# A two-layer FFN and token-mix trunk on one core: sub-layer ends without GpSimd, decay tables on VectorE, preparation spread out

## The chip, the cores and the metric

The kernel runs on one core of a Trainium2 chip. The metric is the device time of one execution in microseconds (us), the median over the runs shown. The engines are TensorE (PE in the rows; PEld is its weight load), VectorE (DVE), ScalarE (ACT), GpSimd (POOL) and SyncE (SP), which here only issues DMAs. The profiled execution is a separate one.

## The reference, cut to what matters

Two layers work on 256 latent tokens and 256 context tokens of width 1024. Each layer is an FFN, a token mix and another FFN; each of the three has a norm before it, a modulation, and a gated residual with a second norm behind it. The vectors of the modulation come from the matrices `w_ada`.

```python
def modulated_norm(xs, gain, mod, s):
    return rms_norm(xs, gain) * (1.0 + mod_vec(mod, 3 * s + 1)) + mod_vec(mod, 3 * s)

def gated_residual(xs, y, gain, mod, s, weight):
    return xs + weight * mod_vec(mod, 3 * s + 2) * rms_norm(y, gain)

def ffn_sublayer(xs, mod, s, g_pre, g_post, w_in_f, w_out_f):
    a, g = jnp.split(modulated_norm(xs, g_pre, mod, s) @ w_in_f, 2, axis=-1)
    return gated_residual(xs, (jax.nn.silu(a) * g) @ w_out_f, g_post, mod, s, MACARON_WEIGHT)
...
for l in range(DEPTH):
    xl = ffn_sublayer(xl, mod_l, 0, ...)          # latents
    xc = ffn_sublayer(xc, mod_c, 0, ...)          # context
    yl, yc = token_mix(modulated_norm(xl, ...), modulated_norm(xc, ...), ...)
    xl = gated_residual(xl, yl, norm_post[l, 1], mod_l, 1, 1.0)
    xl = ffn_sublayer(xl, mod_l, 2, ...)
    if not last:                                  # the last layer's mix and second FFN keep the latents only
        xc = gated_residual(xc, yc, norm_post[l, 1], mod_c, 1, 1.0)
        xc = ffn_sublayer(xc, mod_c, 2, ...)
return xl
```

One of the four branches of the token mix is a state-space model (S5). It needs tables of powers of a complex decay and of their products with the matrices B and C, which depend on the parameters alone, not on the tokens.

## The kernel before

**Tokens and precision.** The tokens lie in four tiles of 128 rows: tiles 0 and 1 are the latents (`st` 0 in the norm), tiles 2 and 3 the context (`st` 1). Every matmul is in three products of a high and a low part (`mm3`, L282 to L287): each operand is split into a part rounded to fp32r and what is left over. The low part is the subtraction `wlo` or `hTlo` in the rows.

**Weights.** `K.W` is a ring (`Ring`): two places for raw weights of 1 MB, loaded from SP's queue, and three places for their halves. `ahead(n)` splits further weights until `n` places ahead are filled: the high half on ScalarE (L208), or on VectorE (L210) if `K.hi_eng` is set; the low half on `K.lo_eng` (L211), which is VectorE except where the end of a sub-layer sets GpSimd. A call of `ahead` thus puts a ScalarE cast and a subtraction into the order of the engines where it stands.

**Order.** Each engine works through its instructions in program order; the order is written out by hand. `K.clock` is a planned clock that the matmul groups advance by `tick`. A `Task` is a generator; its `yield` gives the planned time after which it emits its next stretch. Two tasks matter here: `Ada`, the modulation vectors, and `s5_prep`, the preparation of the S5 tables of a layer during its first FFN. `finish` emits what is left of a task at once.

**The norm before a sub-layer** (`PreNorm`): `square` takes sums of squares on ScalarE, `stats` the reciprocal root, `scale` writes `xs` on VectorE (L433), `transpose` brings it to PSUM on TensorE (L292), and `modulate` applies scale and shift on ScalarE (L459), or on VectorE (L457), casts the high part on VectorE (L462) and subtracts the low part (L463) on the engine that its argument `los` names for each half.

**The end of a sub-layer** (`natural_out`) is the output projection, two column halves wide. In the second half the last weight pieces are held back, so that the tiles end one after the other: `part(ps, s, t)` multiplies one piece for tile t, `first(t)` begins the norm of the result, `update(ts)` finishes the residual and takes the squares for the next norm. The latents' norm is emitted between the context's parts; the context's norm (`ctx_norm`) at the start of the next sub-layer. With two tiles (before the last FFN) the same is done with no context to cover it. `nh` is the number of held pieces, 5 after an FFN and 4 after a mix.

**Preparation** (`s5_discretize` for both layers, within layer 0; `s5_load`; `s5_prep`). `s5_load` issues nine DMAs on two queues, `d1` and `d2`. `s5_prep` then builds, for each group `qg` of four, the table `rt` on VectorE, the table `x` (`p_xr`, `p_xi`) on GpSimd, which TensorE transposes, and for `qg` 0 and 1 the decay table F (`p_F`) in six doubling steps m = 1 to 32, each one complex product (`cmul`, six operations). The tables go to DRAM by DMAs on GpSimd's queue.

**Startup** (in `trace`): the first modulation vectors are computed through `Ada` with the weights in places borrowed from other tiles; the norm of the latents follows, then that of the context.

Stages of the profiled execution: startup to 62 us, first FFN to 469, mix to 910, second FFN to 1320; layer 1: first FFN to 1732, mix to 2014, second FFN (latents only) to the end.

Of the kernel before, what the change touches and what calls it, by code (L numbers as in the profile page):

```python
# [8 lines left out]
F32 = mybir.dt.float32  # L9
# [5 lines left out]
P = 128  # L15
# [450 lines left out]
def natural_out(K, y1, lhi, llo, nk, wview, tiles, G, nxt, hold, free):  # L466
# [55 lines left out]
    for h in range(2):  # L522
# [16 lines left out]
            continue  # L539
        if nxt is not None:  # L540
            pn = nxt()
        lo_eng = K.lo_eng
        if len(tiles) == 2:
            if pn is not None:
                K.lo_eng, K.hi_eng = nc.gpsimd, v
            subs = [piece(i, h, min(K.W.nsub - 1, n - 1 - len(hold) - i)) for i in range(n - nh, n)]
            for t in tiles:
                for j, s in enumerate(subs):
                    part(pss[t], s, t)
                    if t == 1 and pn is not None:  # L550
                        K.W.ahead(min(j, K.W.nsub - 1))
                first(t)
                update([t])
            if pn is not None:
                pn.stats(0)
                for q in range(2):
                    pn.scale(0, q)
                    pn.transpose(0, q)
                for q in range(2):
                    pn.modulate(0, q, (v, nc.gpsimd))  # L560
        else:
            subs = []
            for i in range(n - nh, n):
                subs.append(piece(i, h, min(K.W.nsub - 1, n - 1 - i)))
                part(pss[0], subs[-1], 0)
            K.lo_eng = nc.gpsimd
            first(0)
            update([0])
            for s in subs:
                part(pss[1], s, 1)  # L570
            first(1)
            K.W.ahead(0)
            update([1])
            pn.stats(0)
            pn.scale(0, 0)
            pn.scale(0, 1)
            for s in subs:
                part(pss[2], s, 2)
            K.W.ahead(K.W.nsub - 1)
            first(2)  # L580
            update([2])
            for i, s in enumerate(subs):
                part(pss[3], s, 3)
                if i == nh - 4:
                    pn.transpose(0, 0)
                    pn.modulate(0, 0, (nc.gpsimd, v))
                if i == nh - 3:
                    pn.transpose(0, 1)
                    pn.modulate(0, 1, (nc.gpsimd, v))
            first(3)  # L590
            update([3])
            pn.stats(1)
        K.lo_eng, K.hi_eng = lo_eng, None
    return pn


def ctx_norm(K, pn):

    for h in range(2):
        pn.scale(1, h)  # L600
        pn.transpose(1, h)
    for h in range(2):
        pn.modulate(1, h, (K.nc.vector, K.nc.gpsimd))


class FfnPools:
# [16 lines left out]
def ffn(K, l, s, f, pn, tiles, nxt, jobs, every=(5.0, 7.6), pools=None, prep=False):  # L623
# [8 lines left out]
    with pools.es as es:  # L632
# [29 lines left out]
            nc.vector.tensor_tensor(out=hid(1, 2 * c + n), in0=g[:, :N], in1=hh.bitcast(F32), op=OP.subtract)  # L662

        for i, (c, part, n) in enumerate(blocks):
            if c == 5 and part == 0 and n == 0:
                if ptask is not None:
                    finish(K, ptask)
                pstack.close()
                pb = es.enter_context(K.tc.tile_pool(name=f"hidB{l}{f}", bufs=1))
                hb = [pb.tile([P, 11, N], F32R, tag=f"hb{k}", name=f"hb{k}") for k in range(2)]  # L670
# [287 lines left out]
def s5_discretize(K, pool, sd):  # L958
# [37 lines left out]
    si = small.tile([P, 2, G2], F32, "p_si")  # L996
    fl = lambda t: t.rearrange("p a g -> p (a g)")
    for _ in zip_longest(exp_exact(nc, small, fl(mag), fl(arg[:, 0]), 2 * G2), sincos(nc, small, fl(co), fl(si), fl(arg[:, 1]), 2 * G2)):
        yield 2.5
    for l in range(2):  # L1000
        nc.gpsimd.dma_start(K.r8d[l], mag[:, 1, 16 * l:16 * l + 16])
    yield 2.5
# [65 lines left out]
def s5_prep(K, l, pool, tab, loads=None):  # L1068
# [9 lines left out]
    if l == 0:  # L1078
        yield from s5_discretize(K, pool, sd)
    else:  # L1080
        dq.dma_start(sd, K.sd)
        loads.append(s5_load(K, l, pool, dq, nc.scalar))
        yield 9.0
    sd = sd[:, :, 16 * l:16 * l + 16]
    pw = sd[:, 0:18, :].rearrange("p (m k) g -> p m k g", k=2)
# [38 lines left out]
    for qg in range(4):  # L1124
# [8 lines left out]
        if qg < 2:  # L1133
            g8 = slice(8 * qg, 8 * qg + 8)
            F = T([P, 8, 2, 64], "p_F")
            v.memset(F[:, :, 0, 0:1], 1.0)
            v.memset(F[:, :, 1, 0:1], 0.0)
            for k in range(6):
                m = 1 << k
                bc = lambda c: fms[k][:, c, g8].unsqueeze(2).to_broadcast([P, 8, m])  # L1140
                cmul(*((g_, pool) if m >= 16 else (v, pool)), F[:, :, 0, m:2 * m], F[:, :, 1, m:2 * m], F[:, :, 0, 0:m], F[:, :, 1, 0:m],
                     bc(0), bc(1), [P, 8, m], "p_cmg" if m >= 16 else "p_cmv")
                if k == 3:
                    yield 2.5
            yield 2.5 if qg == 0 else 11.0
            dq.dma_start(tab[:, g8, 640:768], F.rearrange("p g k n -> p g (k n)"))
        else:
            yield 5.0
# [489 lines left out]
def trace(K, nc, tc, rec):  # L1638
# [4 lines left out]
    with ExitStack() as es:  # L1643
# [43 lines left out]
        for l in range(2):  # L1687
# [2 lines left out]
        pn = PreNorm(K, 0, 0)  # L1690
        pools = FfnPools(K, 0, 0, 4, True)
        K.tasks.clear()
        ada = Ada(K, [h[:, 4 * j:4 * j + 4, :].rearrange("p (i a) b -> p i (a b)", i=2) for h in pools.hidden(F32) for j in range(2)],
                  [(0, 0, "norm", None)])
        for i, _ in enumerate(ada.run((0.0, 0.0), mm_tile)):
            if i == 0:
# [13 lines left out]
        pools.loads.append(s5_load(K, 0, pools.prep, nc.sync, nc.sync))  # L1710
        K.clock = 5.0
        for h in range(2):
            pn.modulate(0, h, (nc.gpsimd, nc.vector), (1,))
            K.W.ahead(1 + h)
        for t in range(2, 4):
            for h in range(2):
                pn.square(t, h)
        pn.stats(1)
        K.tasks.append(pools.ptask)
        for l in range(2):  # L1720
            last = l == 1
# [76 lines left out]
```

## Time and profile before

| | us |
|---|---|
| median of three runs | 2229.19 |
| lowest and highest run | 2224.33, 2229.96 |
| profiled execution | 2226.91 |
| its span, first to last instruction | 2225.1 |

The mean granted clock of TensorE over the span is 0.985 of full speed. Times within the span count from its first instruction. Between the profiled execution and its span lie 1.8 us.

### The profile page before, as it was taken

How to read it: one execution, taken by the hardware profiler on the slowest of the kernel's cores; microseconds unless marked ns; L12 is line 12 of the kernel's file. 1: busy time of each engine (PE TensorE's matmuls, PEld its weight loads, DVE VectorE, ACT ScalarE, POOL GpSimd, SP SyncE). 2: the span in 40 equal slices, each digit the busy share in tenths (PEclk: the TensorE clock that was granted, in tenths of full speed). 3: DMA queues.
4: the chain of work that ended last, by engine and by line, in shares of the span. 5: the costliest groups of instructions: out<-in, count | busy, mean ns of one | idle time of the engine just before them, and what ended most of it. 6: DMA issues, size and time to landing. Idle time of an engine off the chain costs nothing.

```text
span 2225.1 us, 28922 instructions
## 1 busy us (share of the span) xinstructions
PE 2120.0 (95%) x11691; PEld 1711.0 (77%) x11691; DVE 1121.9 (50%) x1965; ACT 764.2 (34%) x1275; POOL 391.6 (18%) x364
## 2 busy tenths in 40 slices
PE   5899999989999999899999999999999889997998
PEld 3677778878867778777777887678888778887997
DVE  5984332357435654533333356733324685756554
ACT  3222222332533334422222332222223345454443
POOL 1461000022222300100000026500000234432000
PEclk8999999999999999999999999999999999999999
DMA  8466543334322223355554335643223544443554
GB/s 296 152 218 213 203 148 104 129 109 153 105 72 71 82 73 116 124 174 189 185 183 155 105 110 183 221 147 120 85 86 110 183 149 143 126 142 127 178 190 150
DMA packets 214110, 323.12 MB, mean 145 GB/s; under 512 B 15736, under 2 KB 156664, under 8 KB 213976
## 3 DMA queue, kind: packets, MB, share of 16 engines
q1 hardware_dynamic: 196864, 287.17, 38.7%
q0 software_dynamic: 8432, 27.37, 3.8%
q10 hardware_dynamic: 8680, 6.73, 1.1%
q8 instruction: 92, 1.51, 0.3%
q14 instruction: 42, 0.34, 0.0%
HBM read 307.57 MB, written 14.71 MB: 145 GB/s over the span
## 4 chain that ended last, share of the span: by engine, by line
PE 46%; DVE 7%; issue 2%; ACT 2%; POOL 1%; DMA 1%; ACTq 0%; DVEq 0%; POOLq 0%
PE mm L285 14%; PE mm L287 14%; PE mm L286 14%; PE aux L341 2%; PE aux L292 1%; DVE wlo L211 1%; DVE xs L433 1%; ACT jk L400 1%; DVE at_mx L1415 0%; DVE hTlo L463 0%; DVE hThi L462 0%; ACT at_p L1424 0%; DVE mrg L890 0%; POOL p_F L110 0%; DVE g_tm L1597 0%
## 5 line engine op out<-in xcount | busy, mean ns | idle before, releaser
L285 PE MATMUL mm<-hThi,whi 128*128 128x512 f32 (+1 forms) x1992 | 719.4, 361 | 14.3 <-DVE hThi L462 8.8
L286 PE MATMUL mm<-hTlo,whi 128*128 128x512 f32 (+1 forms) x1992 | 703.4, 353 | 7.2 <-POOL hTlo L463 6.8
L287 PE MATMUL mm<-hThi,wlo 128*128 128x512 f32 (+1 forms) x1992 | 702.0, 352 | 2.0 <-DVE wlo L211 2.0
L211 DVE TENSOR_TENSOR wlo<-wraw,whi 128x1024 fp32r<-128x1024 f32 (+1 forms) x285 | 361.4, 1274 | 422.1 <-ACT whi L208 420.3
L285 PEld LDWEIGHTS mm<-hThi,whi 128*128 128x128 f32 x1992 | 382.4, 192 | 124.5 <-issue 50.3
L208 ACT ACTIVATE whi<-wraw 128x1024 fp32r<-128x1024 f32 (+1 forms) x348 | 363.6, 1048 | 237.1 <-PE mm L287 171.3
L286 PEld LDWEIGHTS mm<-hTlo,whi 128*128 128x128 f32 x1992 | 382.4, 192 | 57.2 <-POOL hTlo L463 9.6
L287 PEld LDWEIGHTS mm<-hThi,wlo 128*128 128x128 f32 x1992 | 382.0, 192 | 53.3 <-DVE wlo L211 2.8
L211 POOL TENSOR_TENSOR wlo<-wraw,whi 128x1024 fp32r<-128x1024 f32 (+1 forms) x66 | 161.3, 2453 | 847.8 <-ACT whi L208 799.0
L655 ACT ACTIVATE sa<-mm 128x512 f32<-128x512 f32 (+1 forms) x88 | 47.8, 543 | 244.7 <-PE mm L287 243.7
L659 DVE TENSOR_TENSOR sa<-sa,mm 128x512 f32<-128x512 f32 (+1 forms) x88 | 54.3, 617 | 151.1 <-PE mm L287 151.1
L285 PE MATMUL mm<-whi,ha 128*128 128x512 f32 x308 | 120.0, 389 | 0.0
L286 PE MATMUL mm<-wlo,ha 128*128 128x512 f32 x308 | 119.8, 389 | 0.0
L287 PE MATMUL mm<-whi,ha 128*128 128x512 f32 x308 | 119.8, 389 | 0.0
L661 ACT ACTIVATE ha<-sa 128x512 fp32r<-128x512 f32 (+1 forms) x44 | 25.4, 578 | 223.9 <-DVE sa L659 223.4
L661 ACT ACTIVATE hb<-sa 128x512 fp32r<-128x512 f32 (+1 forms) x44 | 25.4, 578 | 178.3 <-DVE sa L659 169.8
L287 PE MATMUL mm<-whi,hTlo 128*128 128x512 f32 (+2 forms) x224 | 80.6, 360 | 4.4 <-POOL hTlo L463 4.3
L285 PE MATMUL mm<-whi,hThi 128*128 128x512 f32 (+2 forms) x224 | 81.2, 363 | 3.3 <-DVE hThi L462 3.3
L286 PE MATMUL mm<-wlo,hThi 128*128 128x512 f32 (+2 forms) x224 | 79.5, 355 | 1.2 <-DVE wlo L211 1.2
L388 POOL DMA_DIRECT2D gd<-ev x12 | 7.0, 582 | 388.4 <-ACT whi L208 230.3
L285 PE MATMUL mm<-whi,hb 128*128 128x512 f32 x188 | 73.1, 389 | 0.0
L286 PE MATMUL mm<-wlo,hb 128*128 128x512 f32 x188 | 73.1, 389 | 0.0
(445 smaller groups left out, 2903.2 us busy)
## 6 DMA issues: line engine op xcount, KB each, us to landing
wraw<-in_w_ffn_in_dram SPq DMA_DIRECT2D x88, 1024.0 KB, 5.1
wraw<-in_w_in_dram SPq DMA_DIRECT2D x42, 1024.0 KB, 5.3
wraw<-in_w_ffn_out_dram SPq DMA_DIRECT2D x40, 1024.0 KB, 5.2
adaG<-in_w_ada_dram SPq DMA_DIRECT2D x32, 1024.0 KB, 5.0
aday<-in_w_ada_dram SPq DMA_DIRECT2D x32, 1024.0 KB, 5.0
ha<-in_w_ada_dram SPq DMA_DIRECT2D x8, 1024.0 KB, 7.5
wraw<-in_w_out_dram SPq DMA_DIRECT2D x7, 1024.0 KB
r_tq<-tab SPq DMA_DIRECT2D x8, 768.0 KB, 9.0
```

Source lines behind the costliest of these rows:

```text
L208: K.nc.scalar.activation(h3, r, AF.Copy)
L211: (self.eng or K.lo_eng).tensor_tensor(out=l3, in0=r, in1=h3.bitcast(F32), op=OP.subtract)
L285: mm(out, ahi, bhi, start=first, stop=False)
L286: mm(out, ahi, blo, start=False, stop=False)
L287: mm(out, alo, bhi, start=False, stop=last)
L292: K.nc.tensor.transpose(out, x, K.ident[:n, :n])
L341: nc.tensor.matmul(ps[o:o + 32, :], self.K.sc[:, k + i, :], w[:, i, 512 * b:512 * b + 512], start=k == 0, stop=k == 6, tile_position=(0, o))
L400: K.nc.scalar.activation(jk[:, :src.shape[-1]], src, AF.Square, scale=1.0 / 32.0, accum_out=acc)
L433: K.nc.vector.tensor_scalar(out=xs, in0=K.x[:, 2 * st + t, 512 * h:512 * h + 512], scalar1=self.rst[st][:, t:t + 1], scalar2=None, op0=OP. ...
L655: nc.scalar.activation(sa[:, :N], ps[:, :N], AF.Silu)
L659: nc.vector.tensor_tensor(out=g[:, :N], in0=g[:, :N], in1=ps[:, :N], op=OP.mult)
L661: nc.scalar.activation(hh, g[:, :N], AF.Copy)
```

## The change

At the ends, the low halves of weights and activations are all subtracted on VectorE, and the high halves cast on ScalarE, GpSimd no longer takes part. With four tiles, `ahead(1)` stands after tile 0's update instead of `ahead(0)` after tile 1, and `ahead(nsub - 1)` behind tile 3's update, ahead of the context's statistics, instead of ahead of tile 2's `first`. The latents' transpositions and modulate come at the first two parts of tile 3 (after an FFN they came at the second and third), and tile 2's update behind the first of them. With two tiles, one weight is split during tile 1's second piece and one after the transpositions, where three were split before.

In the preparation, the steps m = 16 and 32 of F move to VectorE; there is a yield after m = 16, and the last yield is 5.0 for qg 0 and 2.5 for qg 1, where it was 2.5 and 11.0. The exponentials and sines of `s5_discretize` take longer yields, `finish` comes three blocks later, and layer 1's `s5_load` issues all of its DMAs on GpSimd's queue, four of which were on ScalarE's. At startup the modulation weights have six places instead of four, the latents' modulate is on ScalarE and VectorE alone, and the preparation's next stretch is due 8 planned us after the context's statistics.

```diff
@@ natural_out, two tiles
-        lo_eng = K.lo_eng
         if len(tiles) == 2:
-            if pn is not None:
-                K.lo_eng, K.hi_eng = nc.gpsimd, v
...
-                    if t == 1 and pn is not None:
-                        K.W.ahead(min(j, K.W.nsub - 1))
+                    if t == 1 and pn is not None and j == 1:
+                        K.W.ahead(0)
                 first(t)
                 update([t])
...
+                K.W.ahead(1)
                 for q in range(2):
-                    pn.modulate(0, q, (v, nc.gpsimd))
+                    pn.modulate(0, q)
@@ natural_out, four tiles
-            K.lo_eng = nc.gpsimd
             first(0)
             update([0])
+            K.W.ahead(1)
             for s in subs:
                 part(pss[1], s, 1)
             first(1)
-            K.W.ahead(0)
             update([1])
...
             for s in subs:
                 part(pss[2], s, 2)
-            K.W.ahead(K.W.nsub - 1)
             first(2)
-            update([2])
             for i, s in enumerate(subs):
                 part(pss[3], s, 3)
-                if i == nh - 4:
-                    pn.transpose(0, 0)
-                    pn.modulate(0, 0, (nc.gpsimd, v))
-                if i == nh - 3:
-                    pn.transpose(0, 1)
-                    pn.modulate(0, 1, (nc.gpsimd, v))
+                if i < 2:
+                    pn.transpose(0, i)
+                    pn.modulate(0, i)
+                if i == 0:
+                    update([2])
             first(3)
             update([3])
+            K.W.ahead(K.W.nsub - 1)
             pn.stats(1)
-        K.lo_eng, K.hi_eng = lo_eng, None
@@ ctx_norm
-        pn.modulate(1, h, (K.nc.vector, K.nc.gpsimd))
+        pn.modulate(1, h)
@@ ffn
-            if c == 5 and part == 0 and n == 0:
+            if c == 5 and part == 1 and n == 1:
                 if ptask is not None:
                     finish(K, ptask)
@@ s5_discretize, loop over exp_exact and sincos
-        yield 2.5
+        yield 5.0
@@ s5_prep, layer 1
-        loads.append(s5_load(K, l, pool, dq, nc.scalar))
+        loads.append(s5_load(K, l, pool, dq, dq))
@@ s5_prep, decay table
-                cmul(*((g_, pool) if m >= 16 else (v, pool)), F[:, :, 0, m:2 * m], F[:, :, 1, m:2 * m], F[:, :, 0, 0:m], F[:, :, 1, 0:m],
-                     bc(0), bc(1), [P, 8, m], "p_cmg" if m >= 16 else "p_cmv")
-                if k == 3:
+                cmul(v, pool, F[:, :, 0, m:2 * m], F[:, :, 1, m:2 * m], F[:, :, 0, 0:m], F[:, :, 1, 0:m], bc(0), bc(1), [P, 8, m], "p_cmv")
+                if k in (3, 4):
                     yield 2.5
-            yield 2.5 if qg == 0 else 11.0
+            yield 5.0 if qg == 0 else 2.5
@@ startup
         ada = Ada(K, [h[:, 4 * j:4 * j + 4, :].rearrange("p (i a) b -> p i (a b)", i=2) for h in pools.hidden(F32) for j in range(2)]
+                  + [pools.gp.tile([P, 2, 1024], F32, tag=t, name="ada" + t) for t in ("G", "y1")],
...
-            pn.modulate(0, h, (nc.gpsimd, nc.vector), (1,))
+            pn.modulate(0, h)
...
         pn.stats(1)
+        pools.ptask.wake = K.clock + 8.0
         K.tasks.append(pools.ptask)
```

## Rows read from the trace of the kernel before

**Rows 1.** The page, part 1: busy time, share and instructions of each engine.
```profile
PE 2120.0 (95%) x11691; PEld 1711.0 (77%) x11691; DVE 1121.9 (50%) x1965; ACT 764.2 (34%) x1275; POOL 391.6 (18%) x364
```
**Rows 2.** Waits of TensorE, whole span: us in sum, count, longest, by releaser.
```profile
PE aux L292 <- DVE xs L433: 21.2, 8, 11.6
...
PE mm L285 <- DVE hThi L462: 12.1, 6, 3.6
...
PE aux L292 <- POOL p_xr L106: 8.5, 1, 8.5
...
PE mm L286 <- POOL hTlo L463: 6.8, 9, 1.0
```
**Rows 3.** Windows; the last three figures: granted clock, DMA share, GB/s.
```profile
22.00:26.00 4.00, 3.57 (x35) 1.28 (x27) 1.51 (x9) 0.60 (x1) 0.00 (x0) 1.00 0.66 208
48.00:58.00 10.00, 6.97 (x45) 6.57 (x44) 8.25 (x25) 3.75 (x8) 1.28 (x1) 0.83 0.47 189
62.00:190.00 128.00, 118.01 (x671) 87.49 (x670) 109.74 (x245) 33.00 (x46) 59.32 (x68) 0.96 0.61 204
462.00:497.00 35.00, 29.32 (x181) 25.84 (x180) 22.95 (x47) 14.32 (x33) 10.53 (x10) 0.95 0.43 142
900.00:930.00 30.00, 24.11 (x160) 20.34 (x162) 20.87 (x46) 13.77 (x36) 7.60 (x5) 1.00 0.19 70
1313.00:1350.00 37.00, 30.32 (x180) 26.99 (x178) 21.51 (x41) 14.84 (x33) 16.86 (x18) 0.82 0.38 114
1390.00:1400.00 10.00, 6.23 (x22) 4.47 (x21) 8.33 (x30) 3.27 (x5) 8.24 (x12) 0.89 0.30 87
2013.00:2035.00 22.00, 9.05 (x51) 7.73 (x51) 15.68 (x26) 8.60 (x21) 11.28 (x7) 0.77 0.16 51
```
**Rows 4.** Timeline of SP's queue at startup: start, us, what, count.
```profile
0.74 22.85 SPq L320 DMA_DIRECT2D ha<-in_w_ada_dram  x8
```
**Rows 5.** Timeline of VectorE at startup.
```profile
49.73 1.52 DVE L84 SCALAR_TENSOR_TENSOR carve<-carve 128x64 f32<-128x64 f32 x6
51.43 1.67 DVE L433 TENSOR_SCALAR xs<-x,pn_rst 128x512 f32<-128x512 f32 x4
```
**Rows 6.** The line L463 by engine, whole span: shortest, median, longest, ns.
```profile
L463 POOL TENSOR_TENSOR hTlo<-h,hThi x22: 1260/1274/1388, 35.6 to 2032.2; 128x512 fp32r<-128x512 f32 x22
...
L463 DVE TENSOR_TENSOR hTlo<-h,hThi x22: 691/693/1648, 37.2 to 2031.1; 128x512 fp32r<-128x512 f32 x22
```
**Rows 7.** Groups of VectorE in 1366 to 1404, shapes apart: busy us, mean ns.
```profile
L104 DVE TENSOR_TENSOR p_F<-p_F,p_sd 128x64 f32<-128x64 f32 x2 | 0.4, 219 | 0.0
```
**Rows 8.** Timeline of VectorE and GpSimd during layer 0's preparation.
```profile
116.58 7.90 DVE L662 TENSOR_TENSOR ha<-sa,ha 128x512 fp32r<-128x512 f32 x1 [0.70 <-ACT ha L661]
...
119.36 1.06 POOL L104 TENSOR_TENSOR p_xr<-p_px,p_B 128x512 f32<-128x512 f32 x1
```
**Rows 9.** Timeline of VectorE and GpSimd at the first FFN's end.
```profile
459.74 5.53 DVE L433 TENSOR_SCALAR xs<-x,pn_rst 128x512 f32<-128x512 f32 x4
...
459.95 4.63 POOL L211 TENSOR_TENSOR wlo<-wraw,whi 128x1024 fp32r<-128x1024 f32 x2 [145.64 <-ACT whi L208]
```
**Rows 10.** Timeline of ScalarE and its queue at the end of layer 0.
```profile
1332.44 3.07 ACTq L1059 DMA_DIRECT2D p_braw<-in_s_b_re_dram  x1
...
1338.69 3.75 ACT L459 ACTIVATE h<-aux,mB,mA 128x256 f32<-128x256 f32 x8 [7.60 <-issue]
```
**Rows 11.** Timeline of VectorE and GpSimd before the last FFN.
```profile
2012.41 4.04 DVE L210 CAST whi<-wraw 128x1024 fp32r<-128x1024 f32 x3
...
2013.25 7.70 POOL L211 TENSOR_TENSOR wlo<-wraw,whi 128x1024 fp32r<-128x1024 f32 x3 [28.78 <-DVE whi L210]
...
2024.96 1.67 DVE L433 TENSOR_SCALAR xs<-x,pn_rst 128x512 f32<-128x512 f32 x4
```
**Rows 12.** Timeline of GpSimd and VectorE during layer 1's preparation.
```profile
1377.00 4.86 POOL L110 TENSOR_TENSOR p_F<-p_F,p_cmgu 128x256 f32<-128x256 f32 x1
...
1388.59 0.07 DVE L1136 MEMSET p_F<- 128x8 f32 x1 [5.31 <-DMA tab<-p_F]
```

More of the change, by code (lines that the diff above doesn't have):

```diff
@@ L1692, in trace @@
         K.tasks.clear()
-        ada = Ada(K, [h[:, 4 * j:4 * j + 4, :].rearrange("p (i a) b -> p i (a b)", i=2) for h in pools.hidden(F32) for j in range(2)],
+        ada = Ada(K, [h[:, 4 * j:4 * j + 4, :].rearrange("p (i a) b -> p i (a b)", i=2) for h in pools.hidden(F32) for j in range(2)]
+                  + [pools.gp.tile([P, 2, 1024], F32, tag=t, name="ada" + t) for t in ("G", "y1")],
                   [(0, 0, "norm", None)])
```

## The prediction, written before the run

> **What bounds the kernel now.** I read the page's totals first [rows 1]: TensorE is busy for 95% of the span, VectorE for half, GpSimd for under a fifth. So a microsecond counts only if TensorE idles in it or runs at the lower clock. The waits of TensorE come next [rows 2]: the large ones are few, and each has one place. 11.6 us go in one piece to the scaled copy `xs` of a pre-norm, 8.5 in one piece to a table that GpSimd computes, 12.1 in six pieces to the high half of the normed activations, 6.8 in nine short pieces to their low half where GpSimd subtracts it. Then the windows, at the places of these waits [rows 3]; the length less PE's busy time is what TensorE idles, and the clock column tells the rest: at the lower of its two levels (1.2 instead of 2.4 GHz) TensorE loses half a microsecond per microsecond, and the time at that level is twice (1 - clock) times the length. The eight windows show what can be won at all: 0.4 in 22 to 26; 3.0 idle and 3.4 at the low clock in 48 to 58; 10.0 idle and 10.2 low in 62 to 190; 5.7 and 3.5 at the end of the first FFN (462 to 497); 5.9 and none after the first mix; 6.7 and 13.3 at the end of layer 0; 3.8 and 2.2 in 1390 to 1400; 13.0 and 10.1 before the last FFN.
>
> **Startup (parts on places, the modulate and the wake).** The eight loads of modulation weights are issued over 22.85 us [rows 4], because with four places the second four wait for matmuls. In 22 to 26 the DMA engines are busy 0.66 of the time [rows 3]; filling that up gives 0.34 x 4 = 1.4, and 0.4 of idle TensorE goes with it: 1.8. Next, the scaling of the context tokens starts at 51.43, right behind the preparation's small operations [rows 5]. The preparation now wakes 8 planned us after the statistics, so those operations fall behind it: 3.0 idle and half of 3.4 go, 4.7. Against that, the latents' modulate moves its GpSimd subtractions to VectorE, 0.69 each instead of 1.27 [rows 6]; the queue of VectorE in front of the context's statistics grows a little, and I take 0.6 off. Startup: 1.8 + 4.1 = 5.9, bounds 3 and 8 (one more stall of 3; all that the two windows hold).
>
> **Preparation, layer 0.** TensorE lost 10.0 idle in 62 to 190, of which 8.5 on the table `p_xr` [rows 2], and it ran low for 10.2, of which 3.9 fall in that idle; half of the other 6.3 is 3.15. Together 13. The tables of qg 1 to 3 stay on GpSimd; the decay table's steps m = 16 and 32 leave it, 24 operations a layer. `x_table(0)` has one yield more and a longer one before its transpositions, 15 planned us instead of 10, so the stall of 8.5 should mostly go. But VectorE gets the operations, and it was already busy 109.74 of 128. Their price is not in the trace at these sizes (128 and 256 elements, 24 of each in both layers). VectorE takes 0.22 for 64 elements [rows 7] and 0.69 for 512 [rows 6]; on a line between them 0.29 and 0.42, so 24 x 0.29 + 24 x 0.42 = 17, half of it in each layer (bounds 10.6 and 33). VectorE's 18.3 idle us in the window hold 8.5, but it is also blocked there: one subtraction of the FFN took 7.90 while GpSimd ran through a table of operations of about 1.06 [rows 8], and these tables stay. I take it that about half of the loss, 7 of 13, comes back; bounds -4 (the 8.5 added, less the bit of slack it finds) and 13.
> One rule bears on this. In [rows 8] VectorE stood for 7.90, through several GpSimd operations. The Trainium skill, "SBUF — State Buffer", section "Who interferes with whom", says that the port pair of the two engines is an exclusive lock and that who issues first has it for the whole instruction, the other being fully blocked. By that, VectorE would wait for at most one GpSimd operation of about 1.1, and the preparation would be free of stalls in the changed order. The trace agrees that one blocks the other, not that it ends with the instruction; I go by the row and keep the other case as a rival.
>
> **Ends with four tiles.** At the first one, the context's scaling takes 5.53 for four operations while GpSimd subtracts two weight halves, 4.63 [rows 9]; alone the four take 1.67 [rows 5]. Both subtractions move to VectorE. A 1,024-element one I price at twice 0.69, 1.4. So the chain from the last matmul to `xs` loses 3.9 of contention and gets one weight half, 1.4, and its ScalarE cast, ahead of the second statistics (`ahead(nsub-1)` moved there). The low halves of the context no longer wait for GpSimd: 1.27 - 0.69 = 0.6 sooner for each second block, about 2 at the last. But TensorE's first wait, from its last matmul over statistics and scaling to the transposition, is latency and stays. I take 1.3 for the end of each layer's first FFN and 2.0 for the end of the first mix, where nothing of the preparation runs beside it; bounds -1 and 3 each. The latents' norm one part sooner costs nothing while the parts of tile 3 cover it: four matmul groups follow each.
>
> **End of layer 0.** ScalarE issues the DMAs of `s5_load` before the context's modulate: two of them took 3.1 each [rows 10] (one is shown, its twin took as long), and the modulate starts at 1338.69 after 7.60 without work. TensorE's longest wait on the high halves is 3.6 [rows 2]. With the issues on GpSimd's queue the modulate starts up to 7 sooner, TensorE wins the 3.6 and half of the low clock that follows that wait, which I put at half of the window's 13.3 [rows 3], so 3.3: 6.9 together, less 2.0 that become visible behind it (the ScalarE cast and the next low halves). 5, bounds 3 and 9. Behind the four issues on GpSimd's queue stand only the preparation's own operations; the first reader comes 9 planned us later.
> A rule speaks against this move: the same page of the Trainium skill, section "SBUF: two separate sides", says that a DMA issued from GpSimd's queue can starve, because the engine writes its descriptors through the port pair that VectorE may hold. No row here shows such an issue beside VectorE at this place. By it the preparation of layer 1 would get its inputs late and lose its gain of 2.5 below, 2199.5 in all.
>
> **Before the last FFN.** From 2012.41 three casts on VectorE take 4.04 and three subtractions on GpSimd 7.70 beside them; `xs` begins at 2024.96, 11 us after TensorE's last matmul [rows 11]. That is the wait of 11.6. Casts go back to ScalarE, one at a time, and one of the three stays ahead of the statistics (j = 1). The 4.0 and some contention in the update before it go: `xs` at about 2020.0, 5 sooner; the low halves, no longer on GpSimd, give 1 more. 6, bounds 4 and 9.
>
> **Preparation, layer 1.** GpSimd needed 4.86 for one addition of the decay table, VectorE then waited 5.31 for the DMA that frees the buffer, and TensorE stood 3.8 in 1390 to 1400 [rows 3, 12]; with half of 2.2 at the low clock it is 4.9. On VectorE the table is ready sooner, with 8.5 more to do there: I take half, 2.5, bounds -2 and 4.9. Two edits move no time by themselves: `finish` three blocks later and the longer yields of `s5_discretize` are hidden by the FFN's matmuls, which don't read them.
>
> **Sum.** 5.9 + 7 + 2 x 1.3 + 2.0 + 5 + 6 + 2.5 = 31. The profiled execution is 2226.91, 2.3 under the median of the runs and inside their spread, so 2226.9 - 31 = 2196; I put 1 on towards the median: 2197. From one measurement to another 0.3%, 6.7 us, is about what can be told from nothing.
>
> **Rivals.** *All stalls of the preparation gone* (the lock ends with each instruction): 13 - 7 and 4.9 - 2.5 more, 8.4, so 2188. For it: VectorE has 18 us free in layer 0's window. Against: the 7.90 of [rows 8].
> *VectorE late*: the preparations give nothing (9.5) and the four-tile ends of FFN and mix nothing (4.6): 31 - 14 = 17, so 2211. For it: moved to VectorE are 17 of decay table, 22 low halves of 0.69 = 15 and some ten weight halves of 1.4 = 14, 46 in all. Against: it is half idle over the span.
> *VectorE held by GpSimd* (slower): each of the eight complex products of the decay table meets a table on GpSimd and is held through six operations of 1.06 = 6.4, 51 in all; if all reaches TensorE, 2197 + 51 = 2248. It decides once more than 38 of the 51, six of eight, get through. Against: eight meetings of eight are unlikely when the extra yields part them.
> *The waits only change their releaser*: TensorE's idle at each end is the latency of the norm, so what is taken off one engine shows on the next; then only the two transfers of startup and of ScalarE's queue count, 2218 to 2229, about 2221.
>
> **How the numbers follow.** Forecast 0.50, with a range of its own of 2189 to 2206; all stalls gone 0.20; VectorE late 0.20; held by GpSimd 0.05; releasers only 0.05. The range leaves out the last two and the tails of the middle ones: the bounds of the two preparations alone make -8 and +16 about 2197, so 2181 to 2214. Faster by over 0.3% (under 2222.5): the first three and nearly half of the last, 0.92; the rest of it, 0.03, is no change; slower 0.05.
>
> **What will show it.** Right: `xs` before the last FFN at some 6 us after the last matmul; no DMA issue on ScalarE at the end of layer 0; no preparation ahead of the context's scaling at startup; the wait on `p_xr` under 3 us; TensorE's busy time unchanged but for the clock. Wrong: a new wait of TensorE on VectorE's decay table or its weight halves in 62 to 190, or the waits on the high halves as long as before.

## The result and the profile after

The changed kernel takes 2196.86 us (median of four runs, 2196.12 to 2197.24), the kernel before beside it 2227.69: ratio 0.986, interval 0.9848 to 0.9872. That is 30.8 us less, against a forecast of 2197 and a sum of 31. The profiled execution's span is 2195.2 where it was 2225.1.

The total came out as forecast, several of its terms did not. To see which, take the end of the same matmul (the same count of the same line and operands) in both traces; before less after is the lead at that place. Matmuls far from an end were taken, since the order of tiles at the ends is changed.

| matmul ends at, before / after | lead | gained since the row above | forecast for that stretch |
|---|---|---|---|
| 85.10 / 75.03, startup over | 10.1 | 10.1 | 5.9 |
| 461.02 / 448.02, layer 0's preparation over | 13.0 | 2.9 | 7 |
| 497.16 / 482.76, first end | 14.4 | 1.4 | 1.3 |
| 895.21 / 882.42, mix | 12.8 | -1.6 | 0 |
| 931.21 / 917.10, end of the first mix | 14.1 | 1.3 | 2.0 |
| 1312.18 / 1298.21, second FFN | 14.0 | -0.1 | 0 |
| 1365.12 / 1344.90, end of layer 0 | 20.2 | 6.2 | 5 |
| 1450.11 / 1425.66, layer 1's preparation | 24.4 | 4.2 | 2.5 |
| 1755.04 / 1729.66, end of layer 1's first FFN | 25.4 | 0.9 | 1.3 |
| 2008.01 / 1982.81, mix | 25.2 | -0.2 | 0 |
| 2036.02 / 2005.58, before the last FFN | 30.4 | 5.2 | 6 |

No edit touches the inside of the first mix, where -1.6 stands: the trace after has the low clock (half speed) for 10.2 us from 786, that of before has none there, and the lead falls by 2.3 at that place. So a step of one or two us in such a table can come from the clock alone.

The page's first part after; it answers to [rows 1]:

```profile
PE 2116.6 (96%) x11691; PEld 1710.9 (78%) x11691; DVE 1116.4 (51%) x2038; ACT 769.3 (35%) x1282; POOL 315.9 (14%) x288
```

VectorE runs 73 instructions more and is busy 5.5 us less. The waits of TensorE, whole span (us in sum, count, longest), beside [rows 2]:

```profile
PE aux L292 <- DVE xs L433: 10.9, 5, 7.6
PE mm L285 <- ACT whi L208: 7.6, 4, 2.6
...
PE mm L285 <- DVE hThi L462: 5.5, 3, 3.3
PE mm L287 <- DVE wlo L211: 4.0, 3, 2.5
...
PE mm L287 <- DVE p_F L1131: 3.3, 1, 3.3
...
PE mm L286 <- DVE hTlo L463: 0.7, 2, 0.3
PE aux L292 <- POOL p_xr L106: 0.6, 1, 0.6
```

The table x cost 8.5 and costs 0.6; the low halves from GpSimd 6.8 and now 0.7 from VectorE; the waits on `xs` and on the high halves (L462, 12.1 before) are halved. The halves of weights rise. Before, the row of `whi`, the high half, was

```profile
PE mm L285 <- ACT whi L208: 3.1, 1, 3.1
```

and that one wait lay in layer 1's preparation. It is gone; the four of 7.6 are new and lie at the four-tile ends (2.6, 1.3, 1.3 and 2.5). The low half `wlo` in the row of L287 goes from 2.0 to 4.0, and a wait of 3.3 on VectorE's decay table is new. The last is not what it says: the wait lies at 108.91 to 112.20, and until 112.14 VectorE was on a weight's low half that TensorE needed.

Windows of the changed kernel (us, busy times by engine, clock, DMA share, GB/s):

```profile
62.00:190.00 128.00, 120.35 (x664) 88.69 (x664) 113.83 (x282) 30.67 (x44) 45.28 (x45) 0.99 0.59 204
62.00:200.00 138.00, 130.35 (x713) 96.19 (x713) 117.67 (x289) 35.31 (x50) 49.70 (x53) 0.99 0.60 206
...
1360.00:1380.00 20.00, 20.00 (x119) 15.39 (x119) 18.14 (x52) 5.85 (x9) 10.46 (x6) 1.00 0.73 250
1988.00:2008.00 20.00, 12.36 (x80) 11.48 (x79) 14.14 (x29) 13.02 (x26) 1.05 (x2) 0.74 0.35 109
```

In the window of layer 0's preparation TensorE still idles 7.7 us, where it was 10.0 [rows 3]. In 1360 to 1380, layer 1's preparation, it doesn't idle at all. Before the last FFN it idles 7.6 in 20 where it was 13.0 in 22 [rows 3].

VectorE in layer 0's preparation, the operations that were long, and GpSimd beside the first of them:

```profile
121.90 7.11 DVE L656 TENSOR_TENSOR ha<-sa,ha 128x512 fp32r<-128x512 f32 x1 [0.70 <-ACT ha L655]
...
149.11 5.76 DVE L1162 TENSOR_TENSOR p_W<-p_W,p_dg 16x64 f32<-16x64 f32 x1
...
164.56 6.63 DVE L656 TENSOR_TENSOR ha<-sa,ha 128x512 fp32r<-128x512 f32 x1 [0.70 <-ACT ha L655]
```
```profile
121.84 1.07 POOL L102 TENSOR_TENSOR p_cmg<-p_px,p_B 128x512 f32<-128x512 f32 x1
...
127.17 1.28 POOL L110 TENSOR_TENSOR p_xi<-p_xi,p_cmgu 128x512 f32<-128x512 f32 x1
```

At these three places, as in [rows 8], an operation of VectorE that starts during a table x on GpSimd is over only when GpSimd's six operations are: the sixth here ends at 128.45, VectorE's at 129.01, and its own share is 0.7. An operation on 16 partitions of 64 elements takes 5.76 that way; the other three of its line in this window take 0.21.

Two of TensorE's waits in this stretch; in the second VectorE comes to the low half only after the last of these operations:

```profile
163.39 1.92 PE L1157 MATMUL aux<-p_rt,p_B 64*16 64x128 f32 x32 [1.91 <-DVE mB L365]
...
172.38 0.50 PE L287 MATMUL mm<-hThi,wlo 128*128 128x512 f32 x1 [2.46 <-DVE wlo L211]
```

Before the last FFN, VectorE's scaling and TensorE behind it, against [rows 11]:

```profile
1995.71 1.68 DVE L433 TENSOR_SCALAR xs<-x,pn_rst 128x512 f32<-128x512 f32 x4
```
```profile
1996.25 3.86 PE L292 MATMUL aux<-ident,xs 128*128 128x128 f32 x16 [7.55 <-DVE xs L433]
```

### The profile page after: what moved, and what is told of

It reads as the page before. It is cut to its first block, busy times and chain, and to the rows that moved or that the text cites. A ratio compares the mean times of both kernels' runs of the same rounds, so it can differ in the third digit from the quotient of the medians.

```text
span 2195.2 us, 28897 instructions
## 1 busy us (share of the span) xinstructions
PE 2116.6 (96%) x11691; PEld 1710.9 (78%) x11691; DVE 1116.4 (51%) x2038; ACT 769.3 (35%) x1282; POOL 315.9 (14%) x288
## 4 chain that ended last, share of the span: by engine, by line
PE 82%; DVE 9%; issue 3%; ACT 3%; DMA 2%; POOL 1%; ACTq 0%; DVEq 0%; SPq 0%; POOLq 0%
PE mm L285 25%; PE mm L286 24%; PE mm L287 24%; PE aux L341 3%; PE aux L292 2%; DVE wlo L211 1%; DVE hTlo L463 1%; PE aux L1434 1%; DMA wraw<-in_w_ffn_in_dram 1%; ACT jk L400 1%; ACT whi L208 1%; PE aux L1559 1%; DVE hThi L462 1%; DVE at_mx L1408 1%; PE aux L1157 1%
## 5 line engine op out<-in xcount | busy, mean ns | idle before, releaser
L287 PE MATMUL mm<-hThi,wlo 128*128 128x512 f32 (+1 forms) x1992 | 699.6, 351 | 7.3 <-DVE wlo L211 4.0
L287 PEld LDWEIGHTS mm<-hThi,wlo 128*128 128x128 f32 x1992 | 379.3, 190 | 59.5 <-DVE wlo L211 5.4
L211 POOL TENSOR_TENSOR wlo<-wraw,whi 128x1024 fp32r<-128x1024 f32 x56 | 138.0, 2471 | 239.9 <-ACT whi L208 223.1
L287 PE MATMUL mm<-whi,ha 128*128 128x512 f32 x308 | 119.8, 389 | 0.0
L655 ACT ACTIVATE ha<-sa 128x512 fp32r<-128x512 f32 (+1 forms) x44 | 25.4, 578 | 244.0 <-DVE sa L653 244.0
L287 PE MATMUL mm<-whi,hTlo 128*128 128x512 f32 (+2 forms) x224 | 79.5, 355 | 0.0
```

Source lines behind the costliest of these rows:

```text
L211: (self.eng or K.lo_eng).tensor_tensor(out=l3, in0=r, in1=h3.bitcast(F32), op=OP.subtract)
L287: mm(out, alo, bhi, start=False, stop=last)
L655: nc.scalar.activation(hh, g[:, :N], AF.Copy)
```

## The experiments

All are the changed kernel with one thing undone or done further, each timed beside the kernel before. "Lost" is against the changed kernel's 2196.86. Where a loss or gain is placed, it was read from the same matmul's end in the trace of the run and in that of the changed kernel. The kernel before, timed beside them in three sessions, had medians of 2225.65 to 2227.75; so a loss of under some 2 us is told by its place in the traces, not by the medians.

**Layer 1's loads on ScalarE's queue again.**
```diff
-        loads.append(s5_load(K, l, pool, dq, dq))
+        loads.append(s5_load(K, l, pool, dq, nc.scalar))
```


> The changed kernel (2196.9) with one part undone: in layer 1, four of the loads of the preparation are issued by ScalarE's queue again. Theory (the prediction's term for the end of layer 0): ScalarE's issue of two loads of some 3 us each stands ahead of the context's modulate, so 5 come back, 2202 (2200 to 2206), with a wait of TensorE on the high halves of about 3.5 near 1317. Rival 1, the gain at that end comes from GpSimd being out of the subtractions, and the issue was hidden: 2196 to 2198. Rival 2, the rule that DMAs from GpSimd's queue starve beside VectorE: the preparation of layer 1 gets its inputs sooner and the kernel is faster, about 2194.

2204.26 (2204.05 to 2205.68), ratio 0.9896 [0.9881, 0.9911]: 7.4 lost. At the end of layer 0 it loses only 2.0. ScalarE issues and TensorE waits so:

```profile
1315.33 0.68 ACTq L1053 DMA_DIRECT2D p_braw<-in_s_b_re_dram  x1
...
1317.43 2.09 ACTq L1055 DMA_DIRECT2D p_craw<-in_s_c_re_dram  x1
1319.57 3.75 ACT L459 ACTIVATE h<-aux,mB,mA 128x256 f32<-128x256 f32 x8 [4.04 <-PE aux L292]
```
```profile
1396.04 0.66 PE L292 MATMUL aux<-ident,p_xr 128*128 128x128 f32 x4 [3.49 <-POOL p_xr L106]
```

The four issues end at 1319.51 and the modulate follows at once, when its transpositions are just done, so no wait on the high halves of 3.5 appears. The other 5.7 are lost at 1392 to 1397, in layer 1's preparation, where TensorE waits for the table x. This is neither the theory's place nor a rival's. The chain to it starts at the loads: the product B, from which x is made, now stands on GpSimd for a load that ScalarE issued.

```profile
1321.27 0.98 POOL L104 TENSOR_TENSOR p_B<-p_braw,p_sd 128x256 f32<-128x256 f32 x1 [9.62 <-DMA p_braw<-in_s_b_re_dram]
```

B is ready at 1325.02, in the changed kernel at 1317.87.

**The old four-tile ends.** The whole branch of `natural_out` and the context's modulate as before.
```diff
             update([0])
-            K.W.ahead(1)
...
             first(1)
+            K.W.ahead(0)
             update([1])
...
-        pn.modulate(1, h)
+        pn.modulate(1, h, (K.nc.vector, K.nc.gpsimd))
```


> The changed kernel (2196.9) with the four-tile ends and the context's norm as before (GpSimd takes the low halves, old order), the rest as changed. Theory by the prediction's terms: 1.3 + 1.3 + 2.0 come back, plus up to 2 at the end of layer 0, where GpSimd took part too: 2201.5 to 2203.5. By the two traces' lead at these ends (2.3, 1.8 and -0.8, and a share of 6.8 at the end of layer 0): 2200 to 2203. Rival, the waits at these ends only change their releaser: 2196 to 2198.

2203.05 (2200.94 to 2203.98), ratio 0.9888 [0.9872, 0.9903]: 6.2 lost by the medians; by the profiled execution (span 2199.2) 4.0. In the traces the startup loses 1.4, the first end 1.5, the end of the first mix 1.3, the end of layer 0 0.4 and that of layer 1's first FFN 0.7; inside the first mix 1.0 comes back, where the low clock lasts 6.8 instead of 10.2. TensorE waits for `xs` 17.0 in seven instead of 10.9 in five, and no more for `whi`. The ends together are near the theory. The startup is not in it: the norm of the context there is undone as well, and TensorE waits for GpSimd's low halves:

```profile
48.75 0.39 PE L286 MATMUL mm<-hTlo,whi 128*128 128x256 f32 x1 [0.42 <-POOL hTlo L463]
...
51.45 0.39 PE L286 MATMUL mm<-hTlo,whi 128*128 128x256 f32 x1 [0.70 <-POOL hTlo L463]
```

**The decay table's large steps on GpSimd again, new yields kept.**
```diff
-                cmul(v, pool, ..., "p_cmv")
+                cmul(*((g_, pool) if m >= 16 else (v, pool)), ..., "p_cmg" if m >= 16 else "p_cmv")
```


> The changed kernel (2196.9) with the decay table's steps 16 and 32 on GpSimd again, all new yields kept. Theory by the prediction: the table on VectorE is a good part of what the two preparations gain (7 and 2.5 were forecast, about 2 and 4 were seen), so 2200 to 2204. Rival, the yields did it and the engine does not matter: 2196 to 2198. Rival, VectorE was loaded for nothing: 2192 to 2195.

2200.61 (2199.33 to 2201.83), ratio 0.9878 [0.9863, 0.9893]: 3.7 lost. In layer 0 it is 1.0 faster than the changed kernel; in layer 1 it loses 5.7, in one wait:

```profile
1395.73 1.12 PE L292 MATMUL aux<-ident,p_xr 128*128 128x128 f32 x4 [5.33 <-POOL p_xr L106]
```

**The old yields, decay table on VectorE.**
```diff
@@ ffn
-            if c == 5 and part == 1 and n == 1:
+            if c == 5 and part == 0 and n == 0:
...
@@ s5_discretize
-        yield 5.0
+        yield 2.5
...
@@ s5_prep
-                if k in (3, 4):
+                if k == 3:
                     yield 2.5
-            yield 5.0 if qg == 0 else 2.5
+            yield 2.5 if qg == 0 else 11.0
```


> The changed kernel (2196.9) with the preparation's yields and the place of finish as before; the decay table stays on VectorE. The run with the table on GpSimd lost nothing in layer 0 and 5.7 in layer 1. Theory: layer 0's gain is that of the yields, so the wait of 8.5 on the table x comes back there, 2201 to 2206. Rival, order and engine only matter together, and either alone is worth little: 2196 to 2199.

2213.39 (2212.72 to 2214.11), ratio 0.9937 [0.9922, 0.9952]: 16.5 lost, far more than either expected. 8.0 are lost by the end of layer 0's preparation and 7.3 in layer 1's. In layer 0 TensorE waits first for the table x and then for operations of ScalarE and VectorE:

```profile
98.38 1.11 PE L292 MATMUL aux<-ident,p_xr 128*128 128x128 f32 x4 [3.03 <-POOL p_xr L106]
100.58 1.11 PE L292 MATMUL aux<-ident,p_xi 128*128 128x128 f32 x4 [1.08 <-POOL p_xi L110]
110.36 1.92 PE L1157 MATMUL aux<-p_rt,p_B 64*16 64x128 f32 x32 [2.65 <-ACT p_xt L1147]
123.38 0.50 PE L287 MATMUL mm<-hThi,wlo 128*128 128x512 f32 x1 [1.03 <-DVE wlo L211]
139.07 0.68 PE L285 MATMUL mm<-hThi,whi 128*128 128x512 f32 x1 [2.47 <-ACT whi L208]
```

Which of the four edits in it counts most was not separated.

**The preparation's wake undone.**
```diff
-        pools.ptask.wake = K.clock + 8.0
```


> The changed kernel (2196.9) without the line that sets the preparation's next stretch to 8 planned us after the context's statistics. Theory by the prediction: the scaling of the context stands behind the preparation's small operations again, 4 come back: 2201 (2200 to 2203). By the two traces the startup gained nearly 10, not 5.9; if the wake is what was mis-sized, 2204 to 2206. Rival, the stall is covered by the weights that are ready now: 2196 to 2198.

2198.24 (2196.57 to 2198.52), ratio 0.9866 [0.9848, 0.9884]: 1.4 lost. The context's scaling starts at 44.63 instead of 41.86, behind the preparation's operations as in [rows 5], but TensorE waits only 0.36 for it: other matmuls cover the 2.8.

```profile
44.63 1.67 DVE L433 TENSOR_SCALAR xs<-x,pn_rst 128x512 f32<-128x512 f32 x4
```
```profile
45.16 2.25 PE L292 MATMUL aux<-ident,xs 128*128 128x128 f32 x16 [0.36 <-DVE xs L433]
```

The trace loses 1.6 by 45, 4.6 more by 115, and has all but 1.6 of it back by 200.

**Four places for the startup's weights.**
```diff
-                  + [pools.gp.tile([P, 2, 1024], F32, tag=t, name="ada" + t) for t in ("G", "y1")],
```


> The changed kernel (2196.9) with four places for the startup's modulation weights instead of six. Theory by the prediction: 1.8 come back, 2198.7. If this is the term that was mis-sized (the startup gained nearly 10 instead of 5.9): 2201 to 2203. Rival, the loads are bound by the DMA engines anyway: 2196 to 2197.5.

2198.93 (2197.68 to 2200.88), ratio 0.9878 [0.9863, 0.9893]: 2.1 lost; the profiled execution has lost 2.8 by 45. TensorE waits 0.6 and 2.5 for loads up to 30.1, where the changed kernel waits 1.4 up to 28.2. The term of 1.8 holds.

**The old startup modulate.**
```diff
-            pn.modulate(0, h)
+            pn.modulate(0, h, (nc.gpsimd, nc.vector), (1,))
```


> The changed kernel (2196.9) with the startup's modulate as before: one block's scaling on VectorE with its subtraction there, the other block's subtraction on GpSimd. The startup gained 9.8 by the traces' lead; places gave 2.0 and the wake 1.4, so theory: this edit, which the prediction booked as a loss of 0.6, holds most of the rest, 5 to 6, 2202 to 2203, with waits of TensorE on GpSimd's subtraction in 33 to 42. Rival, the parts of the startup overlap and none of them is worth more: 2196 to 2199.

2199.77 (2198.59 to 2200.04), ratio 0.9874 [0.9858, 0.9891]: 2.9 lost, all of it by 45. It is not most of the rest, but the sign is against the prediction, which booked the edit as a loss:

```profile
35.08 0.58 PE L286 MATMUL mm<-hTlo,whi 128*128 128x256 f32 x1 [0.90 <-POOL hTlo L463]
38.90 0.58 PE L286 MATMUL mm<-hTlo,whi 128*128 128x256 f32 x1 [0.76 <-POOL hTlo L463]
```

TensorE loses 1.7 there, and in 30 to 50 its mean clock is 0.74 against 0.83.

**The old end before the last FFN.**
```diff
+                K.lo_eng, K.hi_eng = nc.gpsimd, v
...
-                    if t == 1 and pn is not None and j == 1:
-                        K.W.ahead(0)
+                    if t == 1 and pn is not None:
+                        K.W.ahead(min(j, K.W.nsub - 1))
...
-                    pn.modulate(0, q)
+                    pn.modulate(0, q, (v, nc.gpsimd))
```


> The changed kernel (2196.9) with the end before the last FFN as before (three weights split beside it, casts on VectorE, subtractions on GpSimd). Theory by the prediction: 6 come back, 2203; by the lead of the two traces at that place 5, 2202. Rival, the wait is the latency of the norm and the work only fills it: 2196 to 2198.

2202.28 (2199.31 to 2204.2), ratio 0.9891 [0.9876, 0.9906]: 5.4 lost, 5.2 of it at that place; TensorE waits 11.57 for `xs`, as in [rows 2].

**The table x on VectorE too.**
```diff
-        outer(g_, xr, xi, px, B, slice(4 * qg, 4 * qg + 4), "p_cmg")
+        outer(v, xr, xi, px, B, slice(4 * qg, 4 * qg + 4), "p_cmv")
```


> The changed kernel (2196.9) with the table x (eight complex products of six operations) on VectorE instead of GpSimd. Theory, VectorE is held until GpSimd's run of operations ends (7.1, 5.8 and 6.6 us in the trace after, at 121.9, 149.1 and 164.6): on VectorE the six operations cost 6 x 0.67 = 4.0, less than the hold, and the holds go; 2190 to 2195, and VectorE's subtraction in the FFN takes 0.7 everywhere in the preparation. Rival, the port is held for one instruction at most and the long operations have another cause: VectorE gets 33 us more work and the stalls grow, 2199 to 2210.

2188.5 (2188.44 to 2190.23), ratio 0.9833 [0.9816, 0.9849]: 8.4 gained, faster than both kernels. By the traces 4.9 are gained in layer 0's preparation and 1.6 in layer 1's; the other 2 lie where no table is computed, 1.1 of them inside the first mix, where the low clock is 6.8 long instead of 10.2. The window of layer 0's preparation:

```profile
62.00:200.00 138.00, 134.89 (x736) 100.50 (x735) 110.83 (x313) 35.65 (x50) 18.10 (x29) 0.99 0.64 219
```

VectorE has 24 more operations than in the changed kernel's window and is busy 6.8 less. The wait at 169.92 (2.46, on a weight's low half behind the held `ha`) and that of 1.91 at 161.49 are gone. The wait at 109 stays, 3.11. One operation of VectorE is still long, so "everywhere" was not met:

```profile
95.38 3.36 DVE L656 TENSOR_TENSOR ha<-sa,ha 128x512 fp32r<-128x512 f32 x1 [0.70 <-ACT ha L655]
```

It stands behind the product B, six operations of 0.62 to 0.74 on GpSimd that end at 98.17.

**A fill between GpSimd's operations.**
The fill writes 8 elements per partition and reads nothing.
```diff
...
+            g_.tensor_tensor(out=o, in0=a, in1=b, op=op)
+            g_.memset(gap, 0.0)
```


> The changed kernel (2196.9) with a fill of 8 elements per partition on GpSimd behind each of the six operations of the table x; the results are the same. Theory 1, GpSimd's run of operations without a pause keeps VectorE out, and an operation that reads nothing lets it in: the FFN's subtraction on VectorE near 121.9 and 164.6 takes at most 2 us instead of 7.1 and 6.6, and the kernel gains like the table on VectorE, 2189 to 2194. Theory 2, VectorE waits until GpSimd's queue has run empty, whatever the operations are: it takes 7 us and more, 2197 to 2201.

2198.6 (2197.07 to 2201.56), ratio 0.9872 [0.9857, 0.9887]: 1.7 lost. VectorE and GpSimd:

```profile
121.86 7.30 DVE L656 TENSOR_TENSOR ha<-sa,ha 128x512 fp32r<-128x512 f32 x1 [0.70 <-ACT ha L655]
```
```profile
122.80 0.11 POOL L1120 MEMSET p_gap<- 128x8 f32 x1
122.87 1.06 POOL L1119 TENSOR_TENSOR p_cmgu<-p_px,p_B 128x512 f32<-128x512 f32 x1
...
128.55 0.09 POOL L1120 MEMSET p_gap<- 128x8 f32 x1
```

This operation, which reads nothing, does not let VectorE in. It is held 7.30, until the sixth operation ends near 128.6. Theory 1 falls. The next operation starts 0.04 before the record of the fill ends, so GpSimd made no pause; whether a pause would let VectorE in is not shown.

**The last split behind the context's statistics.**
```diff
-            K.W.ahead(K.W.nsub - 1)
             pn.stats(1)
+            K.W.ahead(K.W.nsub - 1)
```


> The changed kernel (2196.9) with the last split of a weight at the four-tile ends behind the context's statistics instead of ahead of them. Theory: the ScalarE cast (0.9) and the subtraction (1.0) stand in the chain from the last matmul to the context's scaling; behind the statistics the cast overlaps them, 0.9 sooner at each of four ends, 2193.5 (2192 to 2195.5). Rival, TensorE then waits as much longer for the high half of that weight: 2196 to 2198.

2196.36 (2194.98 to 2205.32), ratio 0.9874 [0.9853, 0.9895]: no difference that the times show; the profiled execution (span 2193.0) is 2.2 shorter. The waits on `xs` fall from 10.9 to 9.0 and those on `whi` rise from 7.6 to 9.6. The rival fits.

**Together: x and B on VectorE, the last split behind the statistics.**
```diff
+            pn.stats(1)
             K.W.ahead(K.W.nsub - 1)
-            pn.stats(1)
...
-    cmul(g_, pool, B[:, 0], B[:, 1], ..., "p_cmg")
+    cmul(v, pool, B[:, 0], B[:, 1], ..., "p_cmv")
...
-        outer(g_, xr, xi, px, B, slice(4 * qg, 4 * qg + 4), "p_cmg")
+        outer(v, xr, xi, px, B, slice(4 * qg, 4 * qg + 4), "p_cmv")
```


> The changed kernel (2196.9) with the table x and the product B on VectorE and the last split behind the context's statistics. By the single runs, 8.4 and about 0.5 (the profiled executions: 2) add up: 2186 to 2188.5. Rival, the product B (six operations of 0.42) makes VectorE late where the FFN needs it: 2189 to 2192.

2185.97 (2183.93 to 2187.45), ratio 0.9813 [0.9798, 0.9828]: 10.9 gained over the changed kernel and the fastest run here. No operation of VectorE is over 1.3 us in 90 to 180, and the six `ha` there average 0.69 us.

## Why the prediction was right, and where its steps were not

**Startup: the size was off, 10.1 for 5.9.** The places hold (1.8 forecast, 2.1 lost without them). The wake was priced at 4.7, the whole stall of before, and is worth 1.4: once the other edits are in, matmuls cover a scaling that comes 2.8 later. The modulate was booked at -0.6, counted as VectorE's extra queue, and is worth 2.9, because GpSimd's 1.27 against 0.69 [rows 6] was on TensorE's path here. The three sum to 6.4. Another 1.4 is the context's modulate, whose low halves GpSimd subtracted before: the run with the old four-tile ends loses them at 48 to 50, and the prediction has no term for them at the startup. The remaining 2.3 of the lead came from no edit alone. Part of it can be the clock, which stayed low for 6.8 from 31.7 in the changed kernel and for 10.2 there in the runs with four places, the old modulate or the old wake; the run with the old yields, which changes nothing so early, also had 10.2 there and lost 0.7.

**Layer 0's preparation: 2.9 for 7.** The prices of the moved steps were right to a hundredth: VectorE in 110 to 150,

```profile
L103 DVE TENSOR_TENSOR p_cmvu<-p_F,p_sd 128x256 f32<-128x256 f32 x2 | 0.8, 418 | 0.0
...
L103 DVE TENSOR_TENSOR p_cmvu<-p_F,p_sd 128x128 f32<-128x128 f32 x2 | 0.6, 284 | 0.0
```

against 0.42 and 0.29. What failed was the step from these prices to who gains. The 8.5 on the table x did go, but other waits came: 3.3, 1.9 and 2.5. All of them wait for VectorE, and the last two vanish with the table x taken off GpSimd. Moving the decay table gains nothing in layer 0 (it is 1.0 faster on GpSimd); the yields carry the gain, and with the table on VectorE and the old yields 8.0 of the lead are gone, 5 more than this stretch had gained. The sentence that the yields of `s5_discretize` and the later `finish` move no time was not tested by itself; all changed yields together are worth 16.5, more than half of the whole gain.

**The end of layer 0, 6.2 for 5, and layer 1's preparation, 4.2 for 2.5.** At the end of layer 0 the wait that was named did go: TensorE stood 5.2 for the high halves there before, in two waits, and stands 0.6 now; some 3 of smaller waits came in behind it, as the prediction allowed for. But the edit that it credited does not carry the gain alone. Put back, ScalarE's four issues take 4.1 (0.68, 0.67, 0.64, 2.09) instead of the 7.6 of before (0.68, 0.79, 3.07, 3.10), end about when the modulate is due, and cost 2.0 there; the old ends put back cost 0.4 there. The other 3.8 are lost by no single run. It may be that either edit alone is enough for them; this was not run. The move of the loads is worth 7.4 all the same, since 5.7 fall due in the preparation. In the changed kernel GpSimd, which has no subtraction left at the ends (inside the mixes it still takes 56 low halves of weights), issues the loads from 1306.28, and the product B starts at 1313.07:

```profile
1306.28 0.85 POOL L1053 DMA_DIRECT2D p_braw<-in_s_b_re_dram  x1
...
1313.07 0.62 POOL L102 TENSOR_TENSOR p_cmg<-p_braw,p_sd 128x256 f32<-128x256 f32 x1
```

Before, that product started at 1345.25; with the lead of 14 to 20 taken off it is 12 to 18 earlier now. So the gain is one of preparation begun earlier, and with the four loads on ScalarE B is 7 later again. Undoing the loads loses 5.7 here, undoing the table's engine 5.7, undoing the yields 7.3, while the stretch gained 4.2 in all. Undoing any one of them brings waits back (the first two on the table x, the third on weight halves, 1.3, 3.5 and 1.6), so all three are needed to remove them.

**Sums of parts.** For the same reason the eight single losses add up to 45.6, 14.8 more than the 30.8 gained. The forecast's terms were made as if they added. That they hit the total was luck in part: the startup gave 4 more, over its bound of 8, and layer 0's preparation 4 less. The total is no evidence for the terms. One bound was also added up wrongly: -8 and +16 about 2197 make 2189 to 2213, not 2181 to 2214.

**The signs.** Of those for being right, no DMA is issued by ScalarE at the end of layer 0, the preparation stands behind the context's scaling (49.87 against 41.86), the wait on `p_xr` is 0.6, and TensorE is busy 2116.6 instead of 2120.0; `xs` before the last FFN came 7.6 after the last matmul and not some 6. One sign of being wrong came too: new waits on weight halves in 62 to 190, 3.3 and 2.5. The other did not, since the waits on the high halves fell from 12.1 to 5.5.

**The ends.** The four-tile ends were sized well (1.4, 1.3, 0.9 for 1.3, 2.0, 1.3; undone, 1.5, 1.3 and 0.7 are lost). The step that foresaw a weight's cast and subtraction ahead of the statistics as the price is seen in the waits on `whi`; putting them behind the statistics only moves the wait. The end before the last FFN gave 5.2 for 6: `xs` comes 7.6 after the last matmul instead of 11.6 (some 6 was forecast), the casts gone.

**The rivals.** Most of the extra gain of "all stalls gone" (2188) was there to be had, but not by its mechanism: it needs the table x off GpSimd (2188.5, of which 6.5 in the preparations where the rival had 8.4), and the lock of one instruction, on which it rested, is not what the traces show. VectorE stood 7.11 through six instructions of 1.05 to 1.29, and 7.30 with fills between them. The Trainium skill, "SBUF — State Buffer", section "Who interferes with whom", has the pair held for the whole instruction by whoever issues first; the traces agree that one engine blocks the other, but not that the wait ends with that instruction. The Trainium skill, "SBUF — State Buffer", section "SBUF: two separate sides", warns that a DMA from GpSimd's queue starves while VectorE holds the ports that the two share. No such starving shows here: nine issues took 0.59 to 0.85 each from 1306.28 on, and moving four of them back cost 7.4. "VectorE late" was half true, and in layer 0 alone: new waits on VectorE of 3.3, 1.9 and 2.5 took most of the gain there, while the ends kept theirs. "Releasers only" holds for the pair of `xs` and `whi`.

## What to carry to other kernels

Where two engines hold each other up, count what an operation holds, not what it costs: the tables were cheaper on the busier engine (4.1 us for six operations of 0.68 there, against 6 to 7 us for which GpSimd's held it). When several edits feed one wait, undo each of them before you credit any: here three were needed together, and the sum of the single prices overstated the gain by half. A forecast that hits its total still has to be checked stage by stage, by the lead of one trace over the other.

## What the runs showed of the hardware that was not expected

- VectorE's two-input operation is not let in between GpSimd's operations when these follow each other without a break: 7.11, 5.76 and 6.63 us in the changed kernel, 7.30 with a 0.1 us fill between them. With the table on VectorE the two of 7.11 and 6.63 take 0.7. It works the other way too: a GpSimd operation of 1.05 took 5.18 at 1383.48 while VectorE ran seven operations of 0.6 to 0.7 without a break.
- Issuing the same four loads on ScalarE's queue took 0.68, 0.79, 3.07 and 3.10 in the kernel before [rows 10], and 0.68, 0.67, 0.64 and 2.09 in the run that put them back, where GpSimd was done with its half of the loads 6 us before and not 0.6. Why the last ones take longer is not shown.
